# A one-core diffusion step: the second stage's modulation in tiles of 256 columns and four channel blocks

## The chip, the cores and the metric

The kernel runs on one core of one Trainium2 chip. The metric is the device time of one execution in microseconds (us). The core's engines are named as in its profile: PE is TensorE's matmuls, PEld its weight loads, DVE is VectorE, ACT is ScalarE, POOL is GpSimd, and SP is SyncE, which here issues nearly all DMAs.

## The reference

One layer of a diffusion backbone works on 128 context tokens and 512 latent tokens, 1024 channels wide, all in float32. What the change touches is the modulation: a conditioning vector for the latents and one for the context each give six vectors of 1024 (two shifts, two scales, two gates), through one weight matrix of 1024 x 6144.

```python
def _layer(x, cond, p, lb, s0):
    mod = jax.nn.silu(cond) @ p['w_ada'] + p['b_ada']
    sh1, sc1, g1, sh2, sc2, g2 = jnp.split(mod[:, None, :], N_MOD, axis=-1)
    mix, s_out = _token_mixer(x * (1 + sc1) + sh1, p, lb, s0)
    x = _layernorm(DEEPNORM_ALPHA * x + g1 * mix, p['ln1_g'], p['ln1_b'])
    ffn = _swiglu(x * (1 + sc2) + sh2, p['w_ffn_in'], p['w_ffn_out'])
    x = _layernorm(DEEPNORM_ALPHA * x + g2 * ffn, p['ln2_g'], p['ln2_b'])
    return x, s_out
```

The token mixer multiplies all tokens with one wide matrix, runs a convolution, a gated scan over 8 heads (HGRN2) and a gated unit over chunks, and adds the three.

## The kernel before, in words

The kernel runs in stages. The first normalises the tokens, works out sh1 and sc1 and the first products. The second, `seq`, holds the scan's heads: for each pair of heads a product for v (VOp, rows of L221 to L223, tile vps) and for each head products for the two gates, q and g (FOp, rows of L216 to L218, tile mm); every product in float32 is made of three with split operands. Behind each head's q its scan is put on a list of background work (`head_scan`): level by level, ten small matmuls into lv (L810), then VectorE and ScalarE update k and q. Later stages are the convolution, the chunked unit, the output products and the feed-forward part.

Two slices of `w_ada` a type, 512 columns each, make twelve slices. Slices 0 to 3 (sh1, sc1) belong to the first stage. Slices 4 to 11 (g1, sh2, sc2, g2) are spread over the second stage by `ADA_AFTER` (L943): one behind the products of each of the first seven heads, the last at the end. "The first slice" below is slice 4, "the fifth" slice 8, "the last" slice 11.

One such slice is `ada_slice` (L410). `ada_small` (L716) loads 1024 x 512 weights in four tiles of 512 KB from SP's queue (L719); `ada_mm` (L415) multiplies them (L422); `ada_fin` (L426) copies the result to SBUF on ScalarE (ms, L428) and turns it into columns (modcol, L433) or rows (modrow, L439) with the bias added. The conditioning vectors (`sil`) are the stationary operand, 32 columns wide, of which two are used. Channel block kc goes to output strip j = kc % 4, the 32 partitions from 32j on, so a slice uses all four strips twice, and the sum over the strips is made in modcol or modrow. A tile of weights holds two channel blocks of 512 columns: tile 0 serves strips 0 and 1, tile 1 strips 2 and 3, tile 2 again 0 and 1, tile 3 again 2 and 3.

The tiles lie in two buffers (`adw`, bufs=2), which ms and br share. So the loads of tiles 0 and 1 can be out before the slice's turn, and the loads of tiles 2 and 3 wait until the matmuls of tiles 0 and 1 have ended. TensorE's order within the second stage isn't written by hand: the scheduler of the tile framework places the instructions when the program is built. SP issues its DMAs in the order in which they stand; one that waits for a buffer holds those behind it.

The first stage multiplies its four slices in another way, in tiles of four channel blocks and 256 columns (`ada_load`, L475; `mods`, L564, rows of L570).

Of the kernel before, what the change touches and what calls it, by code (L numbers as in the profile page):

```python
# [9 lines left out]
F32 = mybir.dt.float32  # L10
# [7 lines left out]
P = 128  # L18
D = 1024
KC = D // P  # L20
# [23 lines left out]
def bcast_row(dram_row, n=P):  # L44
    return bass.AP(dram_row.tensor, dram_row.offset, [[0, n]] + [list(d) for d in dram_row.ap])
# [3 lines left out]
def hybrid_step(  # L49
# [9 lines left out]
    V_, S_, G_, PE, SP = nc.vector, nc.scalar, nc.gpsimd, nc.tensor, nc.sync  # L59

    w_ada, w_in, w_a_out, w_b_out, w_c_out, w_o, w_ffn_in, w_ffn_out = (
        w[0] for w in (w_ada, w_in, w_a_out, w_b_out, w_c_out, w_o, w_ffn_in, w_ffn_out))
# [75 lines left out]
    loads = []  # L138
# [257 lines left out]
    sil = cst.tile([P, KC, 32], F32, name="sil")  # L396
# [12 lines left out]

    def ada_slice(n, pmp, loads, pool, tag):  # L410

        fin = ada_mm(n, pmp, loads, pool, tag)[1]
        fin()

    def ada_mm(n, pmp, loads, pool, tag):  # L415
        ps = pmp.tile([P, 512], F32, tag="pm", name="mods")
        last = None
        for t, k0, kcs in loads(n):
            for k in range(kcs):
                kc = k0 + k  # L420
                j = kc % 4
                last = PE.matmul(ps[32 * j:32 * j + 32, :], sil[:, kc, :], t[:, k, :],  # L422
                                 start=kc < 4, stop=kc >= 4)
        return last.ins, lambda: ada_fin(n, ps, pmp, pool, tag)

    def ada_fin(n, ps, pmp, pool, tag):  # L426
        ms = pool.tile([P, 512], F32, tag=tag, name="ms", bufs=2)
        S_.copy(ms, ps)  # L428
        ty, hf = n // 2, n % 2
        if ty in MODCOL:  # L430
            pc = pmp.tile([P, 4, 2], F32, tag="pm", name="modcol")
            for q in range(4):
                last = PE.matmul(pc[:, q], ms[:, q * P:(q + 1) * P], sel2, start=True, stop=True).ins  # L433
            bb = bcol[:, ty, hf * 4:hf * 4 + 4].unsqueeze(2).to_broadcast([P, 4, 2])
            V_.tensor_tensor(out=modc[:, MODCOL[ty], hf * 4:hf * 4 + 4], in0=pc, in1=bb, op=ALU.add)
            return last
        else:
            pr = pmp.tile([2, 512], F32, tag="pm", name="modrow")
            PE.matmul(pr, sel2, ms, start=True, stop=True)  # L439
            br = pool.tile([2, 512], F32, tag=tag, name="br", bufs=2)  # L440
            SP.dma_start(br, bcast_row(b_ada[0, n * 512:(n + 1) * 512], 2))
            V_.tensor_tensor(out=br, in0=pr, in1=br, op=ALU.add)
            SP.dma_start(g_scr[(ty - 2) // 3, :, hf * 512:(hf + 1) * 512], br)
# [270 lines left out]
    vp = hgs.enter_context(tc.tile_pool(name="vp", bufs=2))  # L714

    def ada_small(n):  # L716
        for k0 in range(0, KC, 2):
            t = hp.tile([P, 2, 512], F32, tag="adw", name="adaw2", bufs=2)
            SP.dma_start(t, w_ada[k0 * P:(k0 + 2) * P, n * 512:(n + 1) * 512].rearrange(  # L719
                "(k p) n -> p k n", p=P))  # L720
            yield t, k0, 2

    def ada_op(n):
        def f():
            ada_slice(n, pmB, ada_small, hp, "adw")
            yield
        return Call(f)
# [546 lines left out]
    c0, nc_ = PARTS[-1]  # L1274
# [19 lines left out]
    hp = hgs.enter_context(tc.tile_pool(name="hg", bufs=1))  # L1294
# [188 lines left out]
    def bank(name):  # L1483

        i = turn[0]
        turn[0] = (i + 1) % 4
        if i % 2 == 0:
            turn[1] = newaux(name) if i else newps(name)
        return turn[1][:, i % 2]
# [27 lines left out]
    def tl(i, j, e):  # L1517
        dst = (B22, T1, T2, T3, T4)[i]
        return e.tensor_tensor(out=dst[1][:, :, j[0]:j[1]], in0=blocks(*j)[3 + i],  # L1519
                               in1=dst[0][:, :, j[0]:j[1]].bitcast(F32), op=ALU.subtract)  # L1520
# [121 lines left out]
    last = tl(4, J1, V_)  # L1642
# [21 lines left out]
    for part, (c0, HH) in enumerate(PARTS):  # L1664
# [33 lines left out]
        for hf in range(0 if final else 2):  # L1698
            slot = [bank("fo") for _ in range(NT)]
            for k0, kcs in f_kcs(HH):  # L1700
                h, lo = taken()
                for t in range(NT):
                    tsl = slice(t * P, (t + 1) * P)
                    for k in range(kcs):
                        kc = k0 + k
# [7 lines left out]
    for t in range(NT):  # L1713
# [4 lines left out]
        ps = {n0: bank("fo")[:, 0:nn] for n0, nn in cols_}  # L1718
# [89 lines left out]
```

## Time and profile before

| | |
|---|---|
| median of three runs | 1598.36 us (1598.06 to 1599.08) |
| the profiled execution | 1599.31 us, span 1597.5 us |
| granted TensorE clock | 0.994 |
| second stage | about 60 to 490 us of the span |
| modulation's matmuls in it (L422) | 128 records, 605 ns in the median |
| DMA | 148.30 MB, mean 93 GB/s |

The profile is of one execution. A matmul of plain f32 operands leaves two records, one for each pass; those of split operands leave one. Records overlap, since matmuls are pipelined, so what a group costs is read from its start to the start of the instruction behind it. In a timeline row stand the start in us, the length of the whole group, engine, line, operation, output<-inputs, active rows and columns of the array, the output's shape, the count of records, and in brackets an idle time ahead of it with what ended it.

### The profile page before, as it was taken

To read this page: it belongs to the slowest core of one execution; us is meant where nothing else is said; L and a number is where in the kernel's file an instruction comes from. 1 tells how busy PE (TensorE), PEld (TensorE's weight loads), DVE (VectorE), ACT (ScalarE), POOL (GpSimd) and SP (SyncE) were. 2 spreads that over 40 slices of the span, in tenths; PEclk is the share of its full clock that TensorE was granted. 3 is DMA by queue.
4 is the path that set the end of the run, shared out by engine and by line. 5 is a ranking of instruction groups with operands and counts; after the bars stand their busy time and mean duration, and the time that the engine had idled before them with its cause. 6 is when DMAs were issued, how large, how long until landed. Compare 5 with 4: busy or idle time off the path is not lost.

```text
span 1597.5 us, 26110 instructions
## 1 busy us (share of the span) xinstructions
PE 1550.9 (97%) x10846; PEld 1422.4 (89%) x10846; DVE 1148.4 (72%) x1971; ACT 513.5 (32%) x799; POOL 192.3 (12%) x182
## 2 busy tenths in 40 slices
PE   7999999999999999999999999999899999999995
PEld 4988998888887899999999899997788898898984
DVE  5555456565677999988997563377896685685878
ACT  3333333233333221121222343223643243242441
POOL 1120220322300000000002312430000000000014
PEclk9999999999999999999999999999899999999998
DMA  9632333333222322322222123432133222223221
GB/s 321 207 106 87 88 98 100 99 94 100 70 58 81 91 80 67 89 70 78 68 67 67 53 80 106 159 93 66 48 111 119 66 80 98 62 80 93 62 85 66
DMA packets 197014, 148.30 MB, mean 93 GB/s; under 512 B 4945, under 2 KB 174441, under 8 KB 196640
## 3 DMA queue, kind: packets, MB, share of 16 engines
q1 hardware_dynamic: 195984, 145.24, 30.2%
q8 instruction: 85, 1.39, 0.4%
q10 hardware_dynamic: 912, 1.39, 0.2%
q14 instruction: 33, 0.27, 0.1%
HBM read 140.31 MB, written 6.31 MB: 92 GB/s over the span
## 4 chain that ended last, share of the span: by engine, by line
PE 84%; DVE 7%; DMA 5%; ACT 2%; issue 1%; POOL 0%; SPq 0%; ACTq 0%; DVEq 0%
PE mm L216 15%; PE mm L218 15%; PE mm L217 15%; PE fx L1527 3%; PE fx L1529 3%; PE fx L1528 3%; PE lv L810 3%; PE fy L1527 2%; PE fo L221 2%; PE fo L222 2%; PE fo L223 2%; PE fy L1529 2%; PE fy L1528 2%; DMA adaw<-in_w_ada_dram 2%; PE vps L221 2%; PE vps L223 2%
## 5 line engine op out<-in xcount | busy, mean ns | idle before, releaser
L216 PE MATMUL mm<-mH,wh 128*128 128x320 f32 x1280 | 401.8, 314 | 0.0
L217 PE MATMUL mm<-mL,wh 128*128 128x320 f32 x1280 | 396.4, 310 | 0.0
L218 PE MATMUL mm<-mH,wl 128*128 128x320 f32 x1280 | 396.1, 309 | 0.0
L199 ACT CAST wh<-raw 128x1024 fp32r<-128x1024 f32 (+1 forms) x186 | 185.0, 995 | 534.7 <-PE mm L217 358.4
L200 DVE TENSOR_TENSOR wl<-raw,wh 128x1024 fp32r<-128x1024 f32 (+1 forms) x185 | 220.6, 1193 | 140.2 <-ACT wh L199 140.0
L216 PEld LDWEIGHTS mm<-mH,wh 128*128 128x128 f32 x1280 | 240.3, 188 | 9.0 <-issue 5.5
L217 PEld LDWEIGHTS mm<-mL,wh 128*128 128x128 f32 x1280 | 240.4, 188 | 3.6 <-issue 3.6
L218 PEld LDWEIGHTS mm<-mH,wl 128*128 128x128 f32 x1280 | 240.3, 188 | 0.3
L997 DVE SCALAR_TENSOR_TENSOR ca<-hb,convw,ca 128x328 f32<-128x328 f32 x464 | 229.0, 560 | 0.0
L1527 PE MATMUL fy<-mT,wh 128*128 128x320 f32 x264 | 85.1, 323 | 3.8 <-ACT p L1541 2.5
L1529 PE MATMUL fy<-mT,wl 128*128 128x320 f32 x264 | 83.6, 316 | 0.4 <-DVE wl L200 0.4
L1528 PE MATMUL fy<-mT,wh 128*128 128x320 f32 x264 | 83.0, 315 | 0.3 <-DVE mT L1519 0.3
L199 ACT CAST wh<-S 128x1024 fp32r<-128x1024 f32 x43 | 44.9, 1050 | 91.2 <-issue 34.7
L221 PE MATMUL vps<-wh,mH 128*128 128x256 f32 (+1 forms) x200 | 66.6, 334 | 0.0
L200 POOL TENSOR_TENSOR wL<-raw,wL 128x1024 fp32r<-128x1024 f32 (+1 forms) x3 | 6.8, 2280 | 494.1 <-ACT wL L199 489.5
L223 PE MATMUL vps<-wh,mL 128*128 128x256 f32 (+1 forms) x200 | 65.7, 328 | 0.0
L222 PE MATMUL vps<-wl,mH 128*128 128x256 f32 (+1 forms) x200 | 65.5, 328 | 0.0
L200 DVE TENSOR_TENSOR wl<-S,wh 128x1024 fp32r<-128x1024 f32 x43 | 52.6, 1222 | 17.5 <-ACT wh L199 17.5
L754 POOL TENSOR_SCALAR fT<-fT,oml,lb 128x640 f32<-128x640 f32 x16 | 26.1, 1632 | 322.6 <-ACT fT L751 270.2
L832 DVE TENSOR_TENSOR k<-k,t 128x320 f32<-128x320 f32 x40 | 21.8, 546 | 55.1 <-PE lv L810 54.8
L1527 PEld LDWEIGHTS fy<-mT,wh 128*128 128x128 f32 x264 | 50.7, 192 | 8.5 <-ACT p L1541 5.4
L1527 PE MATMUL fx<-mB,wh 128*128 128x320 f32 x176 | 55.1, 313 | 2.0 <-ACT u L1604 1.3
(406 smaller groups left out, 3413.1 us busy)
## 6 DMA issues: line engine op xcount, KB each, us to landing
raw<-in_w_in_dram SPq DMA_DIRECT2D x96, 512.0 KB
adaw<-in_w_ada_dram SPq DMA_DIRECT2D x48, 512.0 KB
raw<-in_w_ffn_in_dram SPq DMA_DIRECT2D x44, 512.0 KB
raw<-in_w_ffn_out_dram SPq DMA_DIRECT2D x20, 512.0 KB
raw<-in_w_b_out_dram SPq DMA_DIRECT2D x8, 512.0 KB
raw<-in_w_c_out_dram SPq DMA_DIRECT2D x8, 512.0 KB
raw<-in_w_a_out_dram SPq DMA_DIRECT2D x8, 512.0 KB
raw<-in_w_o_dram SPq DMA_DIRECT2D x8, 512.0 KB
```

The source lines that it names most:

```text
L199: S_.copy(h, raw)
L200: le.tensor_tensor(out=lo, in0=raw, in1=h.bitcast(F32), op=ALU.subtract)
L216: PE.matmul(ps, h, aH, start=first, stop=False)
L217: PE.matmul(ps, h, aL, start=False, stop=False)
L218: return PE.matmul(ps, lo, aH, start=False, stop=last)
L221: PE.matmul(ps, aH, h, start=first, stop=False)
L222: PE.matmul(ps, aH, lo, start=False, stop=False)
L223: return PE.matmul(ps, aL, h, start=False, stop=last)
L997: paced(V_.scalar_tensor_tensor(out=ca[:, p_], in0=hb[:, p_.start + j:p_.stop + j], scalar=convw[:, k, j:j + 1], in1=ca[:, p_], op0=ALU.mu ...
L1527: PE.matmul(ps, wh, bh, start=kc == 0 and not add, stop=False, skip_group_check=add)
L1528: PE.matmul(ps, wh, bl, start=False, stop=False, skip_group_check=add)
L1529: PE.matmul(ps, wl, bh, start=False, stop=kc == 3, skip_group_check=add)
```

## The change

The four tiles of a slice are cut the other way: 256 columns of four channel blocks instead of 512 columns of two. Their size stays 512 KB; a row of the load is 1 KB instead of 2 KB, and there are 512 instead of 256. Tile 0 holds columns 0 to 255 of blocks 0 to 3, tile 1 the same columns of blocks 4 to 7, tiles 2 and 3 the other 256 columns. Each tile serves all four strips, with four matmuls of 256 columns instead of two of 512. `ada_mm` goes, and its loop stands in `ada_slice`.

```diff
     def ada_slice(n, pmp, loads, pool, tag):
 
-        fin = ada_mm(n, pmp, loads, pool, tag)[1]
-        fin()
-
-    def ada_mm(n, pmp, loads, pool, tag):
         ps = pmp.tile([P, 512], F32, tag="pm", name="mods")
-        last = None
-        for t, k0, kcs in loads(n):
-            for k in range(kcs):
-                kc = k0 + k
-                j = kc % 4
-                last = PE.matmul(ps[32 * j:32 * j + 32, :], sil[:, kc, :], t[:, k, :],
-                                 start=kc < 4, stop=kc >= 4)
-        return last.ins, lambda: ada_fin(n, ps, pmp, pool, tag)
+        for t, c0, k0 in loads(n):
+            for j in range(4):
+                PE.matmul(ps[32 * j:32 * j + 32, c0:c0 + 256], sil[:, k0 + j, :], t[:, j, :],
+                          start=k0 == 0, stop=k0 == 4)
+        ada_fin(n, ps, pmp, pool, tag)
...
     def ada_small(n):
-        for k0 in range(0, KC, 2):
-            t = hp.tile([P, 2, 512], F32, tag="adw", name="adaw2", bufs=2)
-            SP.dma_start(t, w_ada[k0 * P:(k0 + 2) * P, n * 512:(n + 1) * 512].rearrange(
-                "(k p) n -> p k n", p=P))
-            yield t, k0, 2
+        for c0 in (0, 256):
+            for k0 in (0, 4):
+                t = hp.tile([P, 4, 256], F32, tag="adw", name="adaw2", bufs=2)
+                SP.dma_start(t, w_ada[k0 * P:(k0 + 4) * P, n * 512 + c0:n * 512 + c0 + 256].rearrange(
+                    "(k p) n -> p k n", p=P))
+                yield t, c0, k0
```

The scheduler's order moves with it, all of it close to the slices. On TensorE in the first slice, from tile 2 (adaw_971) on, there stood before:

```order
L422 MATMUL mods<-adaw_971,sil 32x512 x2
L217 MATMUL mm<-mL,wh 128x320
L218 MATMUL mm<-mH,wl 128x320
L216 MATMUL mm<-mH,wh 128x320
L217 MATMUL mm<-mL,wh 128x320
L218 MATMUL mm<-mH,wl 128x320
L422 MATMUL mods<-adaw_975,sil 32x512 x2
L810 MATMUL lv<-q_850,k_710 64x64 x10
L439 MATMUL modrow<-ms,sel 2x512
```

In the changed kernel, whose line numbers behind this place are six or seven smaller, the same place (tile 2 is adaw_975, tile 3 adaw_981) reads:

```order
L415 MATMUL mods<-adaw_975,sil 32x256 x4
L217 MATMUL mm<-mL,wh 128x320
L218 MATMUL mm<-mH,wl 128x320
L216 MATMUL mm<-mH,wh 128x320
L217 MATMUL mm<-mL,wh 128x320
L218 MATMUL mm<-mH,wl 128x320
L216 MATMUL mm<-mH,wh 128x320
L217 MATMUL mm<-mL,wh 128x320
L415 MATMUL mods<-adaw_981,sil 32x256 x4
L218 MATMUL mm<-mH,wl 128x320
L804 MATMUL lv<-q_850,k_710 64x64 x7
L432 MATMUL modrow<-ms,sel 2x512
```

Tile 2 stands three mm rows nearer to the pair of tiles 0 and 1, tile 3 one, and modrow stands inside lv: its last three matmuls come behind it. Tiles 0 and 1 stay side by side, and tiles 2 and 3 stay alone. It is so in six of the other seven slices too; in the last slice and in three within the v products tile 2 comes four rows earlier.

In the fifth slice, tile 0 (adaw_3052) was cut in two before, one block at about 267 us, the other at 294 us with tile 1. The late part on TensorE, behind the first products of rmsb, was, with tile 2 adaw_3060 and tile 3 adaw_3064:

```order
L810 MATMUL lv<-q,ks 64x64 x10
L422 MATMUL mods<-adaw_3060,sil 32x512 x2
L810 MATMUL lv<-q_3036,k_2889 64x64
L934 MATMUL rmsb<-rmsH,identr 128x320
L935 MATMUL rmsb<-rmsL,identr 128x320
L934 MATMUL rmsb<-rmsH,identr 128x320
L935 MATMUL rmsb<-rmsL,identr 128x320
L422 MATMUL mods<-adaw_3064,sil 32x512 x2
L810 MATMUL lv<-q_3036,k_2889 64x64 x2
```

It is now, with tile 3 named adaw_3102:

```order
L804 MATMUL lv<-q,ks 64x64 x10
L415 MATMUL mods<-adaw_3102,sil 32x256 x4
L804 MATMUL lv<-q_3068,k_2921 64x64 x6
L928 MATMUL rmsb<-rmsH,identr 128x320
L929 MATMUL rmsb<-rmsL,identr 128x320
L426 MATMUL modcol<-sel,ms 128x2 x4
```

Tile 3 stands where tile 2 stood. Tile 0 and one block of tile 1 have gone to the early place, behind rmsp instead of around it, and the other three blocks of tile 1 stand with tile 2 where one block of tile 0 stood with tile 1.

On SP, the loads of that slice stood before among the other loads as follows:

```order
L719 DMA adaw_3052<-in_w_ada_dram 128x2x512
L174 DMA raw<-in_w_in_dram 128x8x128
L719 DMA adaw_3056<-in_w_ada_dram 128x2x512
L875 DMA out_dram<-fin 128x2x128
L801 DMA s_3530<-in_state_hgrn_dram 128x2x128
L174 DMA raw<-in_w_in_dram 128x8x128 x2
L174 DMA raw<-in_w_in_dram 128x4x256 x2
L719 DMA adaw_3060<-in_w_ada_dram 128x2x512
L719 DMA adaw_3064<-in_w_ada_dram 128x2x512
```

Now the same four loads are adaw_3084, 3090, 3096 and 3102:

```order
L713 DMA adaw_3084<-in_w_ada_dram 128x4x256
L713 DMA adaw_3090<-in_w_ada_dram 128x4x256
L869 DMA out_dram<-fin 128x2x128
L795 DMA s_3578<-in_state_hgrn_dram 128x2x128
L713 DMA adaw_3096<-in_w_ada_dram 128x4x256
L174 DMA raw<-in_w_in_dram 128x8x128 x2
L174 DMA raw<-in_w_in_dram 128x4x256 x2
L713 DMA adaw_3102<-in_w_ada_dram 128x4x256
```

The load of tile 2 has moved ahead of four loads of `w_in`; that of tile 3 has kept its place. On no engine has a row of the later stages moved.

## The prediction

> **What bounds the kernel now.** I read the page's busy shares first, then the table of stretches with the waits of TensorE, then the timeline around the slices that the change rewrites.
>
> ```profile
> PE 1550.9 (97%) x10846; PEld 1422.4 (89%) x10846; DVE 1148.4 (72%) x1971; ACT 513.5 (32%) x799; POOL 192.3 (12%) x182
> ```
>
> ```profile
> core 0: us, PE busy (x) PEld busy (x) DVE busy (x) ACT busy (x) POOL busy (x), PEclk, DMA share, GB/s
> 60.00:490.00 430.00, 424.23 (x3848) 377.75 (x3848) 244.44 (x389) 148.13 (x278) 89.11 (x91) 1.00 0.32 95
> ...
> 490.00:600.00 110.00, 110.00 (x624) 99.79 (x623) 108.20 (x232) 28.56 (x33) 0.84 (x9) 1.00 0.27 78
> ```
>
> ```profile
> PE mods L422 <- DMA adaw<-in_w_ada_dram: 3.8, 7, 2.0
> PE lv L810 <- DVE q L842: 1.1, 2, 0.6
> PE ktp L855 <- DVE k L840: 0.3, 1, 0.3
> ```
>
> TensorE is busy for 97% of the span. In the second stage (about 60 to 490 us) it works 424.23 of 430 us, and its listed waits sum to 5.2 us, 3.8 of them for the modulation's own weights. In the 110 us behind, it does not pause at all. So a microsecond that TensorE saves in the second stage should reach the end: VectorE works 108.20 of 110 us behind it, but on results of TensorE, and starts earlier with them. No step of other engines or of DMA has to become shorter for this. The profiled execution took 1599.31 us with a span of 1597.5; the median of the three runs shown is 1598.36, 0.95 below. I sum against the first and take the difference off the second.
>
> **What one tile costs now.** The timeline of TensorE in the first slice (start, length, line, records; a matmul in f32 leaves two records, one a pass):
>
> ```profile
> 89.20 1.07 PE L422 MATMUL mods<-adaw,sil 128*32 128x512 f32 x8
> 90.19 0.42 PE L216 MATMUL mm<-mH,wh 128*128 128x320 f32 x1
> ...
> 93.86 0.31 PE L216 MATMUL mm<-mH,wh 128*128 128x320 f32 x1
> 94.27 1.05 PE L422 MATMUL mods<-adaw,sil 128*32 128x512 f32 x4
> 95.25 0.41 PE L217 MATMUL mm<-mL,wh 128*128 128x320 f32 x1
> 95.50 0.31 PE L218 MATMUL mm<-mH,wl 128*128 128x320 f32 x1
> 95.65 0.31 PE L216 MATMUL mm<-mH,wh 128*128 128x320 f32 x1
> ...
> 96.18 1.05 PE L422 MATMUL mods<-adaw,sil 128*32 128x512 f32 x4
> 97.16 0.80 PE L810 MATMUL lv<-q,k 128*64 128x64 f32 x20
> ```
>
> Tiles 0 and 1 stand side by side: eight records hold TensorE for 90.19 - 89.20 = 0.99 us. Tiles 2 and 3 stand alone, four records each, and hold it just as long: 95.25 - 94.27 = 0.98 and 97.16 - 96.18 = 0.98. The reader is to see that half the records take the same time. The four output strips of 32 columns (j) run side by side; a tile of two channel blocks fills two strips and leaves two empty, unless its neighbour fills them. The last slice reads the same, as do those at 134.56, 195.30, 240.67, 331.05 and 391.74:
>
> ```profile
> 474.96 1.06 PE L422 MATMUL mods<-adaw,sil 128*32 128x512 f32 x8
> 480.16 1.05 PE L422 MATMUL mods<-adaw,sil 128*32 128x512 f32 x4 [0.42 <-DMA adaw<-in_w_ada_dram]
> 481.92 1.05 PE L422 MATMUL mods<-adaw,sil 128*32 128x512 f32 x4
> ```
>
> **What one tile will cost.** The first stage already multiplies in tiles of four blocks and 256 columns (L570), four of them in a row at 44 us:
>
> ```profile
> 44.06 1.93 PE L570 MATMUL mods<-adaw,sil 128*32 128x256 f32 x32
> 45.93 0.51 PE L648 MATMUL v0a<-wh,mH 128*128 128x256 f32 x2
> ```
>
> ```profile
> 45.38 0.61 PE L570 MATMUL mods<-adaw,sil 128*32 128x256 f32 x8
> ```
>
> Eight records are one such tile: the last one holds TensorE for 45.93 - 45.38 = 0.55 us. The three ahead took (1.87 - 0.55) / 3 = 0.44 each. So a lone tile goes from 0.98 to 0.55, and a neighbouring pair from 0.99 to 0.44 + 0.55 = 0.99: **nothing for the pair, 0.43 us for each lone tile**. In seven slices that is 14 x 0.43 = **-6.0 us**.
>
> The fifth slice is split otherwise:
>
> ```profile
> 267.22 0.62 PE L422 MATMUL mods<-adaw,sil 128*32 128x512 f32 x1
> ...
> 269.27 0.39 PE L221 MATMUL vps<-wh,mH 128*128 128x256 f32 x1
> ```
>
> ```profile
> 294.27 1.06 PE L422 MATMUL mods<-adaw,sil 128*32 128x512 f32 x6
> 299.40 1.05 PE L422 MATMUL mods<-adaw,sil 128*32 128x512 f32 x4 [1.97 <-DMA adaw<-in_w_ada_dram]
> 300.38 0.37 PE L810 MATMUL lv<-q,k 128*64 128x64 f32 x2
> 300.69 0.41 PE L934 MATMUL rmsb<-rmsH,identr 128*128 128x320 f32 x1
> ...
> 301.46 1.05 PE L422 MATMUL mods<-adaw,sil 128*32 128x512 f32 x4
> ```
>
> ```profile
> 471.93 1.28 PE L912 MATMUL rmsp<-sq,onc 128*32 128x512 f32 x16
> 473.15 0.41 PE L217 MATMUL mm<-mL,wh 128*128 128x320 f32 x1
> ```
>
> At 267 one block of tile 0 runs inside rmsp, together 269.27 - 267.22 = 2.05 us; rmsp alone takes 473.15 - 471.93 = 1.22. In the new order tile 0 and one block of tile 1 stand there apart from rmsp: four passes, 0.99, with 0.2 for one more change of work (its price is worked out below), 2.41 in all, **+0.36**. At 294 three blocks and a whole tile take 0.99 as the three blocks did. At the place of tile 2 stands tile 3, 0.55 instead of 0.98 (**-0.43**), and the fourth group at 301.46 is gone (**-0.98**). Together -1.05.
>
> **The waits for the loads.** A pair's end releases the buffers, and tile 2's load starts:
>
> ```profile
> 90.29 0.88 SPq L719 DMA_DIRECT2D adaw<-in_w_ada_dram x2
> ```
>
> From issue at 90.29 to first use at 94.27 are 3.98 us, and TensorE waited there a little; elsewhere it was 0.42 (480.16) or 1.97 (299.40). Tile 0 now ends about one tile ahead of the pair's end, 0.44 us earlier, so its successor's load leaves 0.44 us earlier. In the first slice's order TensorE also comes to tile 2 three matmuls of mm earlier, which start 95.65 - 95.50 = 0.15 us apart: 0.45, a draw. In the four slices where it comes four rows earlier, up to 0.15 more is waited: I put **+0.25 us** for them together. In the fifth slice tile 2's load is now released at 268 instead of 295, behind it only tile 3's is late: released at about 294.27 + 0.44 + 0.2 = 294.9, landed 3.98 later at 298.9, and used where tile 2 was, so 0.5 of the 1.97 us goes: **-0.5**. Bounds: all 3.8 us gone; or the loads leave no earlier while TensorE comes 0.44 earlier in seven slices, +3.1.
>
> Whether the new load takes longer (512 rows of 1 KB instead of 256 of 2 KB, the same 512 KB) is seen from two loads of other weights that ran alone, the first in rows of 1 KB (issued at 81.50), the second in rows of 2 KB (440.82), each in its first 3 us:
>
> ```profile
> 81.50:84.50 3.00, 3.00 (x38) 2.74 (x36) 1.62 (x2) 0.43 (x1) 1.76 (x4) 1.00 0.59 170
> ...
> 440.82:443.82 3.00, 3.00 (x22) 3.00 (x22) 3.00 (x5) 0.74 (x2) 0.00 (x0) 1.00 0.59 173
> ```
>
> 170 x 3.0 = 510 KB against 519: no difference that TensorE would feel, and I take 0; the other bound, half the rate, is the third rival. The number of issues on SP stays at four a slice. [...]
>
> **What the new order adds.** The scheduler cuts lv's ten matmuls around modrow or modcol in three slices where they were whole, and no longer cuts them in one. A cut costs a change of work: the two records at 300.38 hold TensorE until 300.69, 0.31 us, against 0.08 for a tenth of a whole lv (0.80 us, x20). Two cuts more at 0.2 are **+0.4**. The mods copy on ScalarE now has less ahead of modrow to hide behind; from nothing to 0.2 us a slice, taken as nothing, at most +1.6.
>
> **Sum.** -6.0 - 1.05 + 0.25 - 0.5 + 0.4 = **-6.9 us**: 1599.31 becomes 1592.4, and the median 1598.36 becomes **1591.5**. With every wait gone and no further cut it is -6.0 - 1.05 - 3.8 = -10.9, 1587.5; with +3.1 of waits, the cuts and 1.6 for the copies it is -1.9, 1596.4.
>
> **The rivals.**
> - *The loads take the place of the matmuls.* TensorE comes earlier, the data doesn't: -6.0 - 1.05 - 0.5 + 3.1 + 0.4 = -4.05, 1594.3. For it: TensorE waits for tile 2 in most slices already. Against it: the load is tied to tile 0's last matmul, which does end earlier. Chance 0.09.
> - *A lone tile is no cheaper.* If the 0.98 is the entry and the drain of such a group and not its columns, a lone tile of 256 columns costs what it did, and the time stays at 1598.4. For it, the first stage has this row, eight records of 256 columns alone:
>
> ```profile
> 16.06 1.08 PE L570 MATMUL mods<-adaw,sil 128*32 128x256 f32 x8 [1.06 <-DMA adaw<-in_w_ada_dram]
> ```
>
> ```profile
> L606 PE MATMUL xA<-ident,xt x32: 270/273/474, 24.0 to 52.9; 128*128 128x128 f32 x32
> ```
>
>   Against it: around that time everything on TensorE is slow (the transposes of L606, between 24 and 53 us, take 474 ns at most and 273 in the median), and the row at 45.38 shows 0.55. Chance 0.06.
> - *Slower: rows of 1 KB land late.* Tiles 2 and 3 of each slice are multiplied about when they land. If a load of 512 KB came d later, tile 2 would be d later, and tile 3, whose load stands behind it in the queue, d more: 16 d in all. The fastest stretch of the page moves this much:
>
> ```profile
> GB/s 321 207 106 87 88 98 100 99 94 100 70 58 81 91 80 67 89 70 78 68 67 67 53 80 106 159 93 66 48 111 119 66 80 98 62 80 93 62 85 66
> ```
>
>   At 321 GB/s 512 KB take 1.6 us, and at half that rate d = 1.6: 1598.36 - 6.9 + 25.6 = 1617.1. Slower by over 0.2% begins at d = (6.9 + 3.2) / 16 = 0.6 us. Against it stand the 170 and 173 GB/s above. Chance 0.03.
>
> **How the numbers follow.** About 0.2% (3.2 us) is what a measurement of this kernel can tell from no change. The forecast, with its own range of 1588.5 to 1593.5, has 0.80; 0.02 is left for what I don't see. Faster by over 0.2% (under 1595.2): the forecast and most of the first rival, 0.87. Within: the second rival, a part of the first, 0.09. Slower 0.04. The range for 8 in 10 reaches from 1588 (nearly all waits gone) to 1595.5 (the first rival and its copies).
>
> **What would show it.** In the new profile: lone groups of the mods line with eight records of 128x256 and 0.55 us to the next instruction; pairs with 16 records and 0.99; TensorE's wait for adaw at about 3.5 us in total instead of 3.8, and the long one of 1.97 down to about 1.5; TensorE busy some 7 us less. It is wrong if lone groups hold TensorE for about 1 us, if the wait for adaw grows by more than 3 us, or if TensorE saves its 7 us and shows them as new waits for lv or modrow further on.

## The result, and the profile after

| | before | after |
|---|---|---|
| median, first comparison | 1598.21 us (1597.98 to 1599.08, 4 runs) | 1589.77 us (1589.16 to 1589.94, 4 runs) |
| ratio, 95% interval | | 0.9945 [0.9932, 0.9957] |
| profiled execution, span | 1599.31, 1597.5 | 1589.94, 1588.1 |

Two more comparisons, each on another chip or at another time, gave 0.9952 [0.994, 0.9965] and 0.9953 [0.994, 0.9965]. The medians fell by 8.4, 7.9 and 7.7 us; 6.9 had been predicted.

To see where the time went I take the same TensorE instruction in both traces as the border of a stage. The table of stretches of before, cut at 60 and 487 us, gives per row the length, then busy time and (instructions) of PE, PEld, DVE, ACT and POOL, and at the end the granted clock, the busy share of the DMA engines and their GB/s:

```profile
0.00:60.00 60.00, 49.92 (x353) 35.57 (x354) 36.54 (x96) 23.52 (x38) 6.13 (x15) 1.00 0.91 295
60.00:487.00 427.00, 421.23 (x3828) 374.75 (x3828) 242.68 (x386) 145.25 (x273) 88.92 (x88) 1.00 0.32 95
487.00:1597.50 1110.50, 1079.75 (x6669) 1012.06 (x6667) 869.14 (x1489) 344.74 (x488) 97.30 (x79) 0.99 0.27 81
```

The same table of after, cut where the same instructions start:

```profile
0.00:59.10 59.10, 49.16 (x353) 35.33 (x354) 36.52 (x96) 23.53 (x38) 6.08 (x15) 1.00 0.92 299
59.10:478.43 419.33, 415.40 (x3956) 377.63 (x3955) 243.77 (x386) 145.05 (x273) 87.46 (x88) 1.00 0.32 97
478.43:1588.10 1109.67, 1079.75 (x6669) 1012.34 (x6667) 869.00 (x1489) 344.79 (x488) 97.82 (x79) 0.99 0.27 81
```

Of the 9.4 us between the two spans, 7.67 lie in the second stage, 0.90 ahead of it and 0.83 behind it. The second stage splits again: TensorE works 421.23 - 415.40 = 5.83 us less, and stands still 3.93 us instead of 5.77, 1.84 less. The list of waits of after names the most of that second part; before's row had 3.8 us in 7:

```profile
PE mods L415 <- DMA adaw<-in_w_ada_dram: 1.8, 3, 1.2
```

And the timeline of TensorE in the first slice, beside the rows at 89.20 to 97.16 of before:

```profile
88.28 1.07 PE L415 MATMUL mods<-adaw,sil 128*32 128x256 f32 x16
89.28 0.41 PE L216 MATMUL mm<-mH,wh 128*128 128x320 f32 x1
...
92.83 0.64 PE L415 MATMUL mods<-adaw,sil 128*32 128x256 f32 x8
93.39 0.41 PE L217 MATMUL mm<-mL,wh 128*128 128x320 f32 x1
...
94.61 0.64 PE L415 MATMUL mods<-adaw,sil 128*32 128x256 f32 x8
95.18 0.41 PE L218 MATMUL mm<-mH,wl 128*128 128x320 f32 x1
95.52 0.68 PE L804 MATMUL lv<-q,k 128*64 128x64 f32 x14
96.13 1.02 PE L432 MATMUL modrow<-ms,sel 128*2 128x512 f32 x2
```

The pair holds TensorE for 89.28 - 88.28 = 1.00 us as before, a lone tile for 93.39 - 92.83 = 0.56 instead of 0.98. In the fifth slice one group of mods is gone, and the long wait is 1.20 instead of 1.97 us:

```profile
290.79 1.06 PE L415 MATMUL mods<-adaw,sil 128*32 128x256 f32 x14
291.78 0.41 PE L928 MATMUL rmsb<-rmsH,identr 128*128 128x320 f32 x1
...
295.15 0.64 PE L415 MATMUL mods<-adaw,sil 128*32 128x256 f32 x8 [1.20 <-DMA adaw<-in_w_ada_dram]
295.72 0.71 PE L804 MATMUL lv<-q,k 128*64 128x64 f32 x12
```

### The profile page after: what moved, and what is told of

The parts are those of the page before. It is cut to its first block, busy times and chain, and to the rows that moved or that the text cites. A ratio compares the mean times of both kernels' runs of the same rounds, so it can differ in the third digit from the quotient of the medians.

```text
span 1588.1 us, 26365 instructions
## 1 busy us (share of the span) xinstructions
PE 1544.3 (97%) x10974; PEld 1425.3 (90%) x10974; DVE 1149.3 (72%) x1971; ACT 513.4 (32%) x799; POOL 191.4 (12%) x182
## 4 chain that ended last, share of the span: by engine, by line
PE 86%; DVE 7%; DMA 4%; ACT 2%; issue 1%; POOL 0%; ACTq 0%; DVEq 0%
PE mm L216 15%; PE mm L218 15%; PE mm L217 15%; PE fx L1521 3%; PE fx L1523 3%; PE lv L804 3%; PE fx L1522 3%; PE fy L1521 3%; PE fy L1523 2%; PE fy L1522 2%; PE fo L221 2%; PE fo L222 2%; PE fo L223 2%; PE vps L221 2%; PE vps L222 2%; PE vps L223 2%
## 5 line engine op out<-in xcount | busy, mean ns | idle before, releaser
L218 PE MATMUL mm<-mH,wl 128*128 128x320 f32 x1280 | 396.6, 310 | 0.0
L218 PEld LDWEIGHTS mm<-mH,wl 128*128 128x128 f32 x1280 | 240.3, 188 | 1.7 <-issue 1.2
L1523 PE MATMUL fx<-mB,wl 128*128 128x320 f32 x176 | 54.6, 310 | 2.4 <-DVE wl L200 2.4
L1521 PE MATMUL fx<-mT,wh 128*128 128x320 f32 x168 | 54.1, 322 | 2.7 <-ACT wh L199 2.6
```

Of the source, the lines that this page charges most:

```text
L218: return PE.matmul(ps, lo, aH, start=False, stop=last)
L1521: PE.matmul(ps, wh, bh, start=kc == 0 and not add, stop=False, skip_group_check=add)
L1523: PE.matmul(ps, wl, bh, start=False, stop=kc == 3, skip_group_check=add)
```

## The experiments

The question is which part of the change gives what: the four strips, the rows of 1 KB, or the order that the scheduler makes of it. The table gathers what the traces show of the second stage, between the same two instructions in every kernel (us). The last column is TensorE's wait for adaw there; medians stand beside those of before in the same comparison.

| kernel | median (before) | length | busy | wait, times |
|---|---|---|---|---|
| before | 1598.21 | 427.0 | 421.2 | 3.8, 7 |
| before, again | (1599.3) | 428.6 | 422.5 | 4.0, 5 |
| after | 1589.77 (1598.21) | 419.3 | 415.4 | 1.8, 3 |
| after, again | 1591.37 (1599.3) | 419.8 | 415.5 | 2.1, 3 |
| after, third time | 1590.49 (1598.2) | 421.9 | 416.8 | 3.1, 3 |
| old rows, four strips | 1594.78 (1599.3) | 429.1 | 421.4 | 5.6, 6 |
| old rows, four strips, again | one run | 424.0 | 417.0 | 4.6, 5 |
| new rows, two strips | 1595.34 (1599.3) | 425.5 | 422.1 | 0.8, 3 |
| after, eviction's readers later | 1589.18 (1598.45) | 419.7 | 414.7 | 3.0, 4 |
| after, tiles 2 and 3 paired | 1586.67 (1598.45) | 416.3 | 412.9 | none listed |
| the same, again | 1586.78 (1598.2) | 416.2 | 412.7 | 0.3, 1 |
| old tiles, paired | 1590.40 (1598.45) | 420.4 | 416.4 | 1.5, 5 |

### Both kernels once more

Two kernels without any edit, to see how far one trace may be trusted.

> The kernel before, unchanged, for a second profile. The profiled execution of before was 1.1 us above its median, and its TensorE was 0.91 us later than the changed kernel's already at 33 us, ahead of the first changed instruction; behind 485 us another 0.9 us came on top. If both are chance of one execution, this profile shows the first stage within 0.3 us of the changed kernel's and a span of about 1596.5. If they belong to the change, they are there again.

> The changed kernel again, for a second profile and a better interval: about 1589.8 us, some 8.4 us (0.53%) under before. Second stage 7.7 us shorter than in the first profile of before, waits for adaw 1.8 us.

Before took 1599.54 us this time, after 1591.37 in the median. In the trace of after, the second stage is 7.25 us shorter than in the first trace of before, where the first trace of after had 7.67; slice by slice the two agree within 0.3 us. Before, run again, is 1.6 us early at the end of the first stage, with the same code, and 1.6 longer in the second, where its fifth slice met a stretch of lower granted clock (0.92 and 0.91 in the two 10 us from 290 us on; last section). My expectation for it missed: its first stage is 0.7 us from that of after, not 0.3, and its span 1597.8 us, not 1596.5. So the 0.90 us ahead of the second stage are no effect of the change, and a single trace is good to some 1.6 us in the sum, though to a few tenths in most slices.

### Old rows with four strips

The loads are those of before (two blocks of 512 columns, rows of 2 KB); each tile is multiplied as four matmuls of 256 columns on four strips, in the same order on TensorE as after.

```diff
-                PE.matmul(ps[32 * j:32 * j + 32, c0:c0 + 256], sil[:, k0 + j, :], t[:, j, :],
-                          start=k0 == 0, stop=k0 == 4)
+                b, c0 = j % 2, 256 * (j // 2 ^ i // 2)
+                PE.matmul(ps[32 * j:32 * j + 32, c0:c0 + 256], sil[:, 2 * i + b, :], t[:, b, c0:c0 + 256],
+                          start=i % 2 == 0, stop=i % 2 == 1)
...
-                t = hp.tile([P, 4, 256], F32, tag="adw", name="adaw2", bufs=2)
+            t = hp.tile([P, 2, 512], F32, tag="adw", name="adaw2", bufs=2)
```

> The loads as before (two channel blocks of 512 columns, rows of 2 KB), the matmuls as changed: four strips of 256 columns from each tile, two strips on one half of the columns, two on the other. TensorE's order is that of the changed kernel row for row. Theory 'strips' (a lone tile is cheap because it fills all four strips): lone groups 0.55 us, as changed. Theory 'rows' (the load in rows of 1 KB lands sooner when two loads follow each other, 3.7 instead of 4.0 us): the wait for adaw goes from 1.8 back to about 3.5 us, and the time is 1591.5. If the landing has nothing to do with the rows, it is 1589.8 and the load of tile 2 takes 3.7 us here too.

Ratio 0.9978 [0.9967, 0.9989], with nine runs between 1591.9 and 1598.5. The first trace is of the longest run; a second one, of a short run, is told of below. Their lists of waits in the second stage say, in this order:

```profile
PE mods L416 <- DMA adaw<-in_w_ada_dram: 5.6, 6, 2.2
```

```profile
PE mods L416 <- DMA adaw<-in_w_ada_dram: 4.6, 5, 1.7
```

Against 1.8 to 3.1 us in the three traces of after: with TensorE's order the same, rows of 2 KB cost 1.5 to 3.8 us of waiting. I had expected about 3.5 us of waits and 1591.5 us by the theory of the rows; both came out higher. The fifth slice shows how most plainly, since TensorE waits there in every trace. Issue and first use of its last load, in after:

```profile
291.47 0.37 SPq L713 DMA_DIRECT2D adaw<-in_w_ada_dram  x1
295.15 0.64 PE L415 MATMUL mods<-adaw,sil 128*32 128x256 f32 x8 [1.20 <-DMA adaw<-in_w_ada_dram]
```

and in the short run of this kernel:

```profile
291.53 0.37 SPq L713 DMA_DIRECT2D adaw<-in_w_ada_dram  x1
295.66 0.64 PE L416 MATMUL mods<-adaw,sil 128*32 128x256 f32 x8 [1.65 <-DMA adaw<-in_w_ada_dram]
```

The use starts 3.68, 3.59 and 3.61 us behind the issue in the three traces of after, and 4.21 and 4.13 in the two here. In the eighth slice it is 3.72, 3.98 and 3.81 against 4.01 and 4.19.

The seventh slice looks stronger in one trace of each. Its two late loads leave 1.26 us behind a smaller load in both kernels, and TensorE waits for them. The DMA view, in 40 pieces of the 6 us from their issue on (busy tenths of the 16 DMA engines), for after:

```profile
DMA  9999999999437789999999999999998531100000
```

and for the short run of this kernel:

```profile
DMA  9999999999935446696889898999999653222221
```

The same 1.53 MB move in both (one piece is 0.15 us). Where the two loads take over from the smaller one, the engines of after dip for five pieces and are full from the 16th to the 30th, and behind the 35th nothing is left. With 2 KB they dip for longer (pieces 12 to 25 hold many digits from 3 to 8), and two tenths go on to the end of the window. The first tile's use starts 4.26 us behind its issue in after and 5.53 here. But this place scatters: it is 4.38 and 5.55 in the other two traces of after, and 6.09 in the long run here. So the half microsecond of the fifth slice is the safer figure. Worked out from the packets' records between 80 and 485 us: packets of 1 KB took 46 ns in the median in after, those of 2 KB 84 in before, so by the median a byte is no cheaper in short rows. But the slowest twentieth took 58 ns or more in after and 220 or more in before (226 and 196 in the two traces here), and in the mean two packets of 1 KB took 102 ns against 105 for one of 2 KB. Why some long ones take so much longer, and whether these hold up the landing, stays open.

### New rows with two strips

The loads of after; each tile is multiplied in two strips, four matmuls with two of them behind the others, as a tile of before filled 64 of the array's 128 columns.

```diff
-                PE.matmul(ps[32 * j:32 * j + 32, c0:c0 + 256], sil[:, k0 + j, :], t[:, j, :],
-                          start=k0 == 0, stop=k0 == 4)
+                s = j % 2 + k0 // 2
+                PE.matmul(ps[32 * s:32 * s + 32, c0:c0 + 256], sil[:, k0 + j, :], t[:, j, :],
+                          start=j < 2, stop=j >= 2)
```

> The loads as changed (four blocks of 256 columns), each tile multiplied into two strips, two blocks one after the other in each. Theory 'strips': a lone tile holds TensorE for four passes of a strip, 0.99 us, as before the change; 14 lone tiles give 6.0 us back, the fifth slice about 1, and tile 0 ends no earlier than tile 1, so that loads leave 0.4 us later: 1597, at most 1 us either way. Rival 'smaller matmuls' (256 columns are cheaper in themselves, or the load's shape is what counts): 1589.8 as changed.

Ratio 0.9977 [0.9968, 0.9986], 1595.34 us: 1.7 us under the 1597 expected (at most 1 us either way), and far from the rival's 1589.8. Its timeline in the first slice has the lone tile back at 93.76 - 92.77 = 0.99 us, with the same eight records:

```profile
92.77 1.06 PE L416 MATMUL mods<-adaw,sil 128*32 128x256 f32 x8
93.76 0.42 PE L217 MATMUL mm<-mL,wh 128*128 128x320 f32 x1
```

The second stage is busy for 422.1 us. Against the 415.4 of after, in the same order but for the fifth slice, which is in pieces much as before, the strips alone are worth 6.7 us. Against the 421.2 of before it is 0.9 more, which I put down to the new order, its cuts and lone rows. The wait for adaw is only 0.8 us, which I put down to TensorE arriving later (0.99 us a lone tile instead of 0.56) and to the new rows landing sooner (3.6 to 3.7 us in the fifth slice above against 4.1 to 4.2). In the medians each half alone gives some 4 us (1599.3 - 1595.34 here, 4.5 with the old rows) and both together 8. The second stages of the traces show less for a half alone, 1.5 us here and 3.0 in the shorter run of the old rows, and 7.3 to 7.7 for both in its first two traces. (The trace here is of a run of 1593.5 us, and 1.4 us of its lead lie ahead of the stage and 3.0 behind it, where nothing was changed; how much of the 4 us in the median is of that kind isn't known.) The two halves need each other: with four strips TensorE comes sooner to the loads, and only loads that land sooner let it keep all of that (1.8 to 3.1 us of waits for adaw with the new rows, 4.6 and 5.6 with the old).

### The eviction's readers two levels later

The loads and strips of after; modrow and modcol come later in the program, with an order (no wait) behind the last matmul of lv, so that lv isn't cut in slices 1 and 3.

```diff
-        ada_fin(n, ps, pmp, pool, tag)
+        pend.append([LEVELS, lambda: ada_fin(n, ps, pmp, pool, tag)])
...
+                    lv_last[0] = PE.matmul(lv[b:b + 64, i], k(i * P + b), q(i * P, b), start=True, stop=True).ins
+            late(1)
```

> Everything of the changed kernel stays; in the order of the program the eviction's readers (modrow or modcol) come two recurrence levels later, so that TensorE runs lv x10 in one piece before them in slices 1 and 3 (no cut 7|3), and behind lv x10 in slice 4; slices 2, 6, 7 and 8 as in the changed kernel, the fifth cut at another place. Theory 'cuts cost': in the changed kernel lv and modcol of slice 3 take 1.97 us where before's took 1.67, and a lone L218 between them 0.34 where it took 0.15, so about 0.4 to 0.5 us come back in each of slices 1 and 3 and 0 to 0.3 in slice 4: 0.8 to 1.3 us less than the changed kernel, about 1589.3 where that is 1590.3 on the same chip. Theory 'cuts are hidden' (something else ends the stretch): within 0.3 us of the changed kernel. Waits for adaw as in the changed kernel, about 2 us in both.

Ratio 0.9942 [0.9929, 0.9955], a second stage 7.29 us shorter than before's: the same as after within what a trace can tell. The cut itself is real. After, third slice, then this kernel at the same place:

```profile
200.14 0.68 PE L804 MATMUL lv<-q,k 128*64 128x64 f32 x14
200.75 1.05 PE L426 MATMUL modcol<-sel,ms 128*128 128x2 f32 x8
201.74 0.45 PE L804 MATMUL lv<-q,k 128*64 128x64 f32 x6
202.11 0.41 PE L216 MATMUL mm<-mH,wh 128*128 128x320 f32 x1
```

```profile
199.99 0.80 PE L819 MATMUL lv<-q,k 128*64 128x64 f32 x20
200.72 1.05 PE L439 MATMUL modcol<-sel,ms 128*128 128x2 f32 x8
201.64 0.40 PE L216 MATMUL mm<-mH,wh 128*128 128x320 f32 x1
```

lv and modcol take 202.11 - 200.14 = 1.97 us in two pieces and 1.65 in one: a cut costs 0.32, not 0.2. TensorE's busy time falls by 0.7 in all, and the wait for adaw in the seventh slice, which has the same order in both kernels, is 1.12 instead of 0.36. My expectation of 0.8 to 1.3 us was too high, and what it did win was within the spread of the waits.

### Tiles 2 and 3 as a pair

After, with tiles 2 and 3 put behind the second lv level, so that the scheduler sets them side by side in slices 1, 2, 3, 4 and 7.

```diff
-        for t, c0, k0 in loads(n):
...
-        ada_fin(n, ps, pmp, pool, tag)
+        it = loads(n)
+        mm([next(it), next(it)])
+        got = list(it)
+
+        def rest():
+            mm(got)
+            ada_fin(n, ps, pmp, pool, tag)
+
+        pend.append([LEVELS, rest])
```

> The changed kernel's tiles, with tiles 2 and 3 of a slice put behind the second recurrence level after tiles 0 and 1 and so next to each other in slices 1, 2, 3, 4 and 7 (27 to 48 rows behind the first pair instead of 18 to 21 and 7 to 9 more); slices 6 and 8 as they were, the fifth in other pieces. Theory 'lone strips and waits': two lone tiles of 0.56 become one pair of 1.00, which is 0.1 a slice; one change of work less, about 0.2 a slice; the wait for adaw in these slices goes (about 0.2 to 0.4 each, 1 to 1.5 in all); no cut of lv, 0.8 to 1.3. Together 2.5 to 4 us less than the changed kernel: 1586 to 1588. Rival 'the later eviction is late' (modrow, modcol and the next loads leave later): no gain, or the fifth slice loses what the others win: 1589.5 to 1592. Waits for adaw: by the first theory under 1.3 us in all, in the fifth slice alone.

Ratio 0.9927 [0.9914, 0.9941]: 1586.67 us. The second pair of the first slice:

```profile
95.96 1.07 PE L418 MATMUL mods<-adaw,sil 128*32 128x256 f32 x16
96.96 0.41 PE L216 MATMUL mm<-mH,wh 128*128 128x320 f32 x1
```

1.00 us for two tiles instead of twice 0.56, one change of work less, no cut of lv, and no wait for adaw. It was run beside after on one chip as well:

> The changed kernel beside e9_pairs_beside on one chip, with the same runs of the kernel before. From its earlier runs: 8 to 9 us under the kernel before, ratio 0.994 to 0.9955, waits for adaw in the second stage about 2 us in 3, no stretch of the second stage with a granted clock under 0.98.

> The kernel of e6_pairs again, for a comparison with the changed kernel on one chip. Its first trace was 3.1 us shorter than that of the changed kernel in the second stage (10.7 against 7.7 under the kernel before) and 2 us shorter behind it, where none of its instructions differ. Theory 'only the second stage counts': 3 us under the changed kernel, 1.5 to 4.5 with the spread of the runs. Rival 'the first comparison was chance between chips': within 1 us of the changed kernel.

After 1590.49 us, ratio 0.9953 [0.994, 0.9965]; pairs 1586.78, 0.9926 [0.9913, 0.994]: 3.7 us apart. The second stage of the pairs measures 416.3 and 416.2 us in the two traces, 3 us under the first two of after. The difference lies in the range of 1.5 to 4.5 us that was expected, and the rival of chance between chips falls. This is the fastest version run here. For after my expectation missed: it is 7.7 us under before instead of 8 to 9, and its trace has 3.1 us of waits and a stretch of lower granted clock (0.93 and 0.90 in the two 10 us from 290 us on), told of at the end.

### The tiles of before as pairs

The order of the pairs with the tiles and rows of before (two strips a tile). The lines differ so from those of the pairs:

```diff
-                    i = PE.matmul(ps[32 * j:32 * j + 32, c0:c0 + 256], sil[:, k0 + j, :], t[:, j, :],
-                                  start=k0 == 0, stop=k0 == 4).ins
+                    i = PE.matmul(ps[32 * j:32 * j + 32, :], sil[:, k0 + k, :], t[:, k, :],
+                                  start=k0 < 4, stop=k0 >= 4).ins
```

> The kernel before's tiles (two channel blocks of 512 columns, rows of 2 KB, two strips of TensorE to a tile) in the order of e6_pairs: tiles 2 and 3 next to each other in slices 1, 2, 3, 4 and 7. Theory 'only a lone tile pays for idle strips': a pair fills the four strips in either shape, 1.00 us; so this kernel loses to e6_pairs only 0.43 us for each tile that still stands alone (two each in slices 6 and 8, three or four pieces of the fifth): 1.7 to 3.5 us, and ends at 1588 to 1591, close to the changed kernel and 7 to 10 us under the kernel before. Rival 'the tile's shape or its rows gain by themselves' (loads, weights, the shorter moving operand): it stays near the kernel before, 1594 to 1598. Waits for adaw under 1.5 us.

Ratio 0.9949 [0.9936, 0.9961], 1590.40 us: as fast as after, without the change's tiles. In slices 1 to 4 it wins 4.8 us against before, the pairs with the new tiles 5.3. It falls behind where its tiles stand alone: by 1.5 to 1.8 us in slices 6 and 8 together, and in the seventh slice, where it can't keep the pair together:

```profile
391.36 1.05 PE L419 MATMUL mods<-adaw,sil 128*32 128x512 f32 x4 [0.49 <-DMA adaw<-in_w_ada_dram]
392.65 1.05 PE L419 MATMUL mods<-adaw,sil 128*32 128x512 f32 x4 [0.25 <-DMA adaw<-in_w_ada_dram]
```

Two waits split it, and each half pays the full 1 us. So the strips can be filled by either way, and the change's tile is the one that needs no neighbour; what its rows of 1 KB add in the order of after is shown above, under the old rows with four strips.

### Old rows, run again

> The kernel of e1_old_rows once more (old loads with rows of 2 KB, four strips of 256 columns), for its second profile. Theory 'a long wait for adaw lowers TensorE's clock': in the first profile the granted clock stood at 0.86 and 0.63 between 290 and 310 us, behind a wait of 1.7 us in the fifth slice, and the run took 1598.5; the timed runs fell in two groups, 1592 to 1595 and 1597.6 to 1598.5. If this run takes 1592 to 1595 its granted clock is above 0.97 in all stretches of 10 us of the second stage; if it takes over 1597 there is again a stretch at 0.9 or less behind a wait for adaw. Rival: the time of the run and the granted clock behind the waits have nothing to do with each other. Either way the waits for adaw are 4.5 to 6 us, against 2 in the changed kernel.

1592.33 us, and the granted clock was 0.91 and 0.92 in the two stretches of 10 us from 290 us on. The theory in this form failed: the short run has such a stretch too. What sets the long run apart is how long it lasted, some 10 us instead of 3.4, and that a second one, of 3.4 us, stands there at 400 us behind a wait of 2.19.

## Why the prediction was right

The time came out at 1589.8 against 1591.5, inside the range; the mechanism was the one named, and two terms were off in size, in opposite directions: TensorE's work in the second stage fell by 0.8 us less than summed, and its waits by 1.6 us more. That the stage came as near to the sum as it did (7.7 us against 6.9) owes something to luck.

- **"Nothing for the pair, 0.43 us for each lone tile"**: right. 0.98 became 0.56 or 0.57, 0.41 less, which is 5.8 us in 14 tiles; the pair stayed at 1.00, and two strips with the new loads bring 0.99 back. Two strips cost 6.7 us in that kernel; 14 x 0.43 and one such tile in the fifth slice are 6.45.
- **The fifth slice, -1.05 and -0.5 of its wait**: right, a little small. The slice is 2.05 us shorter, 0.77 of it the wait (1.97 to 1.20).
- **The waits, +0.25 in the other slices**: the step that failed most. I costed the new loads by two loads that ran alone and found 510 and 519 KB in 3 us, "no difference that TensorE would feel". But these loads run beside others, and there the new rows land sooner: in the fifth slice they are used 3.6 to 3.7 us behind the issue, where rows of 2 KB in the same order take 4.1 to 4.2 and the prediction took 3.98 for both. In all, TensorE's standing still in the second stage fell by 1.84 us instead of 0.25. The three traces of after have 3.93, 4.25 and 5.17 us of it and the two of before 5.77 and 6.11, so about 1.5 is the fairer figure; 0.8 of it is the fifth slice's wait, and the others fell by 0.7 instead of rising by 0.25. By the median packet the short rows are the dearer (2 x 46 = 92 ns against 84), in the mean the cheaper (102 against 105).
- **The cuts, +0.4**: too small. TensorE's work fell by 5.83 us, where the terms without waits (-6.0, -1.05, +0.4) make -6.65. With 5.8 us for the tiles and 1.28 for the fifth slice (2.05 - 0.77), the new order adds 1.2 us instead of 0.4. Two cuts at 0.32 are 0.6 of it. The prediction left out that a lone L218 now stands between tile 3 and lv in the first and third slices, where tile 3 was followed by lv at once: 95.52 - 95.18 = 0.34 us for one that costs 0.15 among its kind, 0.2 in each. The rest isn't taken apart.
- **The copies of mods, nothing**: no wait for ms is among TensorE's waits of after, and moving its readers two levels away won nothing beyond the cut.
- **The path**: "a microsecond that TensorE saves in the second stage should reach the end" held. What lies behind the stage is 0.83 us shorter with the same busy time, 1079.75. Run again, before has 1110.8 us there and after 1109.8, as was expected of an effect of the change. But in the third trace of after TensorE stands still for 30.9 us behind the stage, and in the first of before for 30.8. So I don't count it to the change, and its cause isn't settled.

Of the rivals, that the loads take the place of the matmuls and that rows of 1 KB land late are refuted by the shorter waits, and that a lone tile is no cheaper by the 0.56.

## What to carry to other kernels

Where a matmul uses a quarter of the array's columns (32 of 128 here), count what stands beside it when it is issued, not what the slice uses in all: a group that filled two of four strips cost as much here as a full one (0.98 us against 1.00) unless its neighbour filled the rest. Pairing such groups in time gave as much as cutting the tile so that it fills the array by itself; both together gave the most here (1586.7 us). Judge a load's form among the loads beside which it runs: alone, the two forms moved the same (510 and 519 KB in 3 us), and beside others they were some 0.5 us apart in the fifth slice.

## What the runs showed of the hardware

In four of these traces TensorE's granted clock dropped in the fifth slice, behind pauses of 1.14 us (third trace of after), 1.65 and 1.74 (old rows, short and long run) and 1.93 (before, run again). In the long run of the old rows with four strips, the granted clock (the number ahead of the DMA share) reads:

```profile
290.00:300.00 10.00, 8.27 (x83) 0.86 0.44 118
300.00:310.00 10.00, 10.00 (x48) 0.63 0.29 95
310.00:320.00 10.00, 10.00 (x98) 1.00 0.08 22
```

and its timeline ahead of and in that stretch:

```profile
297.04 1.05 PE L416 MATMUL mods<-adaw,sil 128*32 128x256 f32 x8 [1.74 <-DMA adaw<-in_w_ada_dram]
...
304.06 0.47 PE L218 MATMUL mm<-mH,wl 128*128 128x320 f32 x1
304.32 0.47 PE L216 MATMUL mm<-mH,wh 128*128 128x320 f32 x1
...
308.05 0.31 PE L217 MATMUL mm<-mL,wh 128*128 128x320 f32 x1
308.19 0.30 PE L218 MATMUL mm<-mH,wl 128*128 128x320 f32 x1
```

Matmuls that start every 0.145 us start every 0.265. In the traces of before and after the granted clock is 1.0 or 0.5, with nothing between (0.50 in each single microsecond from 1142 to 1147 us of before); taken as 0.5 here too, an estimate, (0.14 + 0.37) x 10 / 0.5 = 10 us by the first two rows passed at half clock. From the group at 297.04 to the pair of the sixth slice it is 34.6 us here and 30.25 in the first two traces of after, in the same order on TensorE: some 4 us lost behind a pause of 1.74. In the fifth slice such a stretch stands in four of the eight traces with a pause of 1.1 us or more there, and in none of the four with less than 0.5. It doesn't follow the pause alone: before had 1.97 us without it and, run again in the same order, 1.93 us with it. No run sets the pause by itself, so that it is the cause isn't shown. In these four traces the stretch cost 1.4 to 4.3 us on top of the wait. If the pause is the cause, a change that shortens it may gain more than the list of waits shows.

In three of the four it lasted about 3.4 us (298.2 to 301.6 in the short run of the old rows). What sets this length, and what makes the clock drop, was not shown.

The same stands behind the second stage: between 1097.5 and 1187.5 us of before the granted clock is 0.94 (0.5 for 6.83 us from 1141.11 on and for 3.41 us from 1154.77 on), in after too (the same two lengths), and 0.98 in the first trace of the pairs at the same instructions. With it go 2.2 us against before that this trace won behind the second stage (1108.3 us instead of 1110.5), where none of its instructions differ. The third trace of after has the same 1108.3, and the second of the pairs 1109.7, so this belongs to neither kernel; the pairs' gain over after is better read from the second stage, 3 us.
